# All value products and projections of ten loops as 64-row pairs

## The chip, the cores and the metric

One core of one Trainium2 chip runs the kernel. The metric is the device time in microseconds of one execution; the time before is 328.2 us, the median of three runs (327.85 to 329.61).

## What is computed

Self-attention over a batch of 32 sequences of different lengths, 8 heads of 64 channels, 512 channels in all. Rows past a sequence's length stay zero.

```
batch, max_seq, n_heads, head_dim = (32, 512, 8, 64)
for b in range(batch):
    x_b = x[b, :lengths[b]]
    q, k, v = np.split(np.matmul(x_b, w_qkv), 3, axis=-1)   # then by heads
    scores = scale * np.matmul(q, k.transpose(0, 2, 1))
    attn = softmax(scores)                                  # over the keys
    output[b, :lengths[b]] = np.matmul(attn, v)
```

## The kernel before

The sequences are sorted on the chip by length and taken two at a time. For each width N in `LOOPS` (512, 448, then 384 down to 96 in steps of 32) there is a loop; it takes the pairs whose longer sequence fits in N columns, so the lengths decide how often each body runs. A body has two positions, j = 0 and 1, one for each sequence of the pair. With the lengths of these inputs the loops from 512 to 96 run 1, 1, 1, 3, 1, 1, 1, 2, 1, 2, 1 and 1 times. n = ceil(N/128) is the number of 128-row tiles of a sequence.

A position does two things at once: the attention of its own sequence and the projections of the next one. Their order is written out by hand in `ORDER`, one string for each loop, with a bar between the two positions. A step's digit after "@" names PSUM banks (there are eight), and letters behind a colon name the engine of each copy out of PSUM: "a" is ScalarE (ACT), "d" is VectorE (DVE); a star says the same as "a". The steps are:

- `S#`: one group of scores, keys by queries. A head has 64 channels, so two heads are multiplied as a pair: two matmuls with 64 contraction rows each, on the upper and the lower half of the TensorE array, into two banks (line 1269; in the loop of 448 also 1259). ACT then takes the exponential of both banks in one instruction (line 1287).
- `B#a`, `B#b`, `B#c`: projections of q and k. The 128 contraction rows are cut in halves; the two halves of a column block go as a pair into two banks, first one way round, then the other, so that both banks get both halves (`halves`, line 1323). The copies follow the last part (line 1367).
- `U#a`, `U#b`: values of two tiles in the same manner (copies at line 1386). `V#a`, `V#b`: values of one tile, its 512 columns in two halves (copies at 1400). `W#a`, `W#b`: the same for the last half tiles of both sequences together.
- `Q#`, `K#`, `V#`, `W#` without a letter behind: projections with all 128 contraction rows in one matmul (`project`, line 300; `values`, line 311; `last_values`, line 1210).
- `A#` without a letter: the product of exponentials and values, 128 rows at once, 65 columns (64 channels and the row sum), `av`, line 1517 (line 1583 in the loops of 128 and 96, `at_once`). DVE then takes the reciprocal of the sums, sets dead rows to zero and scales: R, U, O at lines 1706, 1712, 1715. `Z#` (line 1557) adds the last half tile, as pairs.
- `A#a`, `A#b`: `paired`, line 1631. Two value products go together, each cut in 64-row halves, into two banks, in two rounds. Where the two banks are neighbours, `both_normed` does one R, U, O for both (lines 1671, 1680, 1693).
- `L`: DVE marks the live rows. `P`: DVE writes a mask and POOL casts the sequence after the next to 16 bits (line 371, n instructions). `D`: SyncE (SP) loads a later sequence into the buffer that the cast has read. `X`: SP transposes the cast sequence by DMA (line 328, n transfers); it waits for the projections of its own position, since it writes the buffer that they read, and the position after the next reads it. `E0` (`columns_left`): projections of columns left over when a loop runs again; its copies are replaced by a memset (line 1479) in a loop's last pass.

Instructions run in order on each engine. `plan_waits` works out the semaphore waits from what each step reads and writes; `op.skip < 0` marks `E0`.

Of the kernel before, what the change touches and what calls it, by code (L numbers as in the profile page):

```python
# [18 lines left out]
P = 128  # L19
# [21 lines left out]
def plan_waits(head, bodies, entries, rare):  # L41
# [22 lines left out]
    def follow(chain):  # L64
        clock = defaultdict(lambda: defaultdict(int))
        seen = defaultdict(list)
        write, readers = {}, defaultdict(list)
        ahead = chain[0] == "head"
        came = -1 if ahead else chain[0]
        for at, v in enumerate(chain):  # L70
# [10 lines left out]
            for w, j, k, op in todo:  # L81
                b = -1 if v == "head" else 2 * (at - ahead) + (j or 0)
                mine = clock[op.eng]
                if op.skip and op.eng == "PE":
                    mine = defaultdict(int, mine)
# [64 lines left out]
                    learn(o)  # L150
                by = op.name if op.dma else op.eng
                count = (seen[by][-1]["count"] if seen[by] else 0) + 1
                after = dict(mine)
                after[by] = count
                o = {"name": op.name, "by": by, "count": count, "clock": after, "b": b}
                o |= {"dma": op.dma, "entry": j is None, "skip": bool(op.skip) and op.eng != "POOL" and not op.passed, "order": len(seen["all"])}
# [5 lines left out]
                    readers[r].append(o)  # L162
                for r in op.writes:
                    write[r] = o
                    readers[r] = []

    follow(["head"])
    for v in range(len(bodies)):
        follow([v, v, v])
        for u in reversed(range(v)):  # L170
            follow([u, v, v])
        follow(["head", v, v])
# [4 lines left out]
def kernel(  # L177
# [9 lines left out]
    B, MAXS, D = x.shape  # L187
# [15 lines left out]
    def ring(n, shape, dtype, name, pool=const):  # L203
# [32 lines left out]
    LOOPS = [512, 448, *range(384, 64, -32)]  # L236

    ORDER = {
# [40 lines left out]
    }  # L279

    NARROW = (512, 448, 384, 320, 288, 256, 192, 128)
# [1620 lines left out]
    def op_of(v, j, k):  # L1902
        return head[k] if v == "head" else (entries[v] if j is None else bodies[v][j])[k]
# [57 lines left out]
    for (v, j, k), todo in waits.items():  # L1961
        op = op_of(v, j, k)
# [81 lines left out]
    with tc.tile_critical():  # L2044
# [38 lines left out]
        for v, N in enumerate(LOOPS):  # L2083
# [17 lines left out]
            body, after = f"loop_{N}", f"after_{N}"  # L2101
            nc.br_lt(pair, ends[v], on_true=body, on_false=after)
            with nc.body(body):
# [6 lines left out]
                for j in range(2):  # L2110
                    for e in EN:
                        mine = [(k, op) for k, op in enumerate(bodies[v][j]) if op.eng == e]
# [54 lines left out]
```

## Time and profile before

| | us |
|---|---|
| median of the runs | 328.2 (327.85 to 329.61) |
| span of the profiled execution | 328.5 |
| PE busy | 311.6 |
| ACT busy | 262.6 |
| DVE busy | 197.7 |
| POOL busy | 101.9 |

Stretches of the span, from the first exponential of one loop to that of the next: 512 from 23.1 to 59.7, 448 to 93.0, 384 to 118.1, 352 (three passes) to 190.4, 320 to 211.7, 288 to 232.8, 256 to 247.4, 224 (two passes) to 275.5, 192 to 288.3, 160 (two passes) to 310.5, then 128 and 96 to the end. Before 23.1 the weights are loaded and cast, the lengths sorted and the first sequence projected.

How to read it: PE is the matmul itself and PEld its weight load, which runs beside other matmuls. Matmuls are pipelined, so the mean time of one is its latency, and the rate is read from the starts in the timeline or from the pieces of the chain that ended last. Shapes such as 64*128 are contraction rows by weight columns.

### The profile page before, as it was taken

To read this page: it belongs to the slowest core of one execution; us is meant where nothing else is said; L and a number is where in the kernel's file an instruction comes from. 1 tells how busy PE (TensorE), PEld (TensorE's weight loads), DVE (VectorE), ACT (ScalarE), POOL (GpSimd) and SP (SyncE) were. 2 spreads that over 40 slices of the span, in tenths; PEclk is the share of its full clock that TensorE was granted. 3 is DMA by queue.
4 is the path that set the end of the run, shared out by engine and by line. 5 is a ranking of instruction groups with operands and counts; after the bars stand their busy time and mean duration, and the time that the engine had idled before them with its cause. 6 is when DMAs were issued, how large, how long until landed. Compare 5 with 4: busy or idle time off the path is not lost.

```text
span 328.5 us, 13310 instructions
## 1 busy us (share of the span) xinstructions
PE 311.6 (95%) x5092; PEld 202.3 (62%) x5092; DVE 197.7 (60%) x635; ACT 262.6 (80%) x413; POOL 101.9 (31%) x148
## 2 busy tenths in 40 slices
PE   6899999999999999999999999999998999999980
PEld 4444645555655556556656657667777886777860
DVE  6777567566666646456455465545575565776853
ACT  4379999897878988988978989899867779687761
POOL 6448040324030330330231243043222224435320
PEclk9999999999999999999999999999999999999997
DMA  6984749395858999696676766857459857966651
GB/s 217 382 278 80 251 140 327 76 354 153 304 52 298 224 269 258 197 268 224 233 214 224 255 194 205 211 174 242 156 131 227 183 176 164 223 206 177 193 180 66
DMA packets 69449, 68.85 MB, mean 210 GB/s; under 512 B 40720, under 2 KB 40720, under 8 KB 69392
## 3 DMA queue, kind: packets, MB, share of 16 engines
q1 hardware_dynamic: 69344, 68.12, 71.4%
q8 instruction: 33, 0.54, 0.7%
q14 instruction: 24, 0.20, 0.2%
q10 hardware_dynamic: 48, 0.00, 0.0%
HBM read 25.17 MB, written 33.55 MB: 179 GB/s over the span
## 4 chain that ended last, share of the span: by engine, by line
PE 84%; DVE 5%; DMA 3%; issue 2%; ACT 2%; SPq 1%; POOL 1%; DVEq 0%; POOLq 0%; ACTq 0%
PE banks L1323 41%; PE banks L1269 13%; PE banks L1517 12%; PE banks L300 6%; PE banks L311 6%; PE banks L1631 2%; DMA xT<-x 2%; DMA x_nat<-in_x_dram 2%; PE banks L1210 1%; PE banks L1557 1%; DVE out_nat L1715 1%; DVE rcp L1712 1%; DVE out_nat L1693 1%; SPq L328 1%; ACT et L1287 1%
## 5 line engine op out<-in xcount | busy, mean ns | idle before, releaser
L1287 ACT ACTIVATE et<-banks 128x704 f16<-128x704 f32 (+8 forms) x256 | 198.8, 825 | 27.8 <-PE banks L1269 24.7
L371 POOL TENSOR_TENSOR x<-x_nat,mask 128x512 f16<-128x512 f32 x83 | 84.2, 1041 | 184.3 <-DVE mask L1052 174.9
L1323 PE MATMUL banks<-xT,w_r 64*128 64x352 f16 (+9 forms) x1536 | 127.8, 294 | 1.8 <-DMA xT<-x 1.2
L1323 PEld LDWEIGHTS banks<-xT,w_r 64*128 64x128 f16 x1536 | 68.7, 94 | 39.0 <-PE banks L1323 8.5
L1269 PE MATMUL banks<-qz,kT 64*128 64x352 f16 (+11 forms) x624 | 77.5, 294 | 2.6 <-issue 0.7
L1715 DVE TENSOR_TENSOR out_nat<-banks,rcp 128x256 f32<-128x256 f32 (+1 forms) x110 | 53.0, 482 | 3.8
L1367 DVE CAST qz<-banks 128x448 f16<-128x448 f32 (+6 forms) x47 | 26.4, 561 | 45.2 <-PE banks L1323 44.8
L1517 PEld LDWEIGHTS banks<-v_aug,et 128*128 128x128 f16 x1240 | 41.7, 97 | 13.5 <-issue 6.8
L1517 PE MATMUL banks<-v_aug,et 128*128 128x65 f16 x1240 | 47.1, 194 | 0.0
L1323 PE MATMUL banks<-w_r,xT 64*128 64x512 f16 (+1 forms) x368 | 46.6, 372 | 0.3 <-ACT v_aug L1489 0.3
L1269 PEld LDWEIGHTS banks<-qz,kT 64*128 64x128 f16 x624 | 28.1, 93 | 25.9 <-issue 7.1
L1706 DVE RECIPROCAL rcp<-banks 128x4 f32<-128x4 f32 (+1 forms) x112 | 20.3, 181 | 20.7 <-PE banks L1517 7.3
L311 PE MATMUL banks<-w_r,xT 128*128 128x512 f16 x104 | 26.9, 381 | 0.5 <-DVE xT L782 0.5
L1386 DVE CAST v_aug<-banks 128x512 f16<-128x512 f32 x25 | 16.6, 690 | 17.9 <-PE banks L1323 17.9
L1323 PEld LDWEIGHTS banks<-w_r,xT 64*128 64x128 f16 x368 | 17.2, 94 | 14.1 <-PE banks L1323 1.0
L1367 ACT CAST kT<-banks 128x352 f16<-128x352 f32 (+6 forms) x47 | 22.5, 479 | 1.5 <-PE banks L1323 1.5
L300 PE MATMUL banks<-xT,w_r 128*128 128x160 f16 (+3 forms) x256 | 23.0, 243 | 0.5 <-DVE v_aug L1489 0.5
L1367 DVE CAST kT<-banks 128x352 f16<-128x352 f32 (+5 forms) x33 | 17.9, 552 | 7.7 <-PE banks L1323 7.6
L300 PEld LDWEIGHTS banks<-xT,w_r 128*128 128x128 f16 x256 | 16.6, 98 | 5.2 <-DMA xT<-x 0.6
L1367 ACT CAST qz<-banks 128x352 f16<-128x352 f32 (+6 forms) x33 | 15.3, 465 | 3.7 <-PE banks L1323 3.6
L1489 ACT CAST v_aug<-banks 128x512 f16<-128x512 f32 x15 | 8.8, 589 | 9.5 <-PE banks L311 9.5
L1631 PE MATMUL banks<-v_aug,et 64*128 64x65 f16 x624 | 14.2, 190 | 0.6 <-issue 0.6
(116 smaller groups left out, 193.3 us busy)
## 6 DMA issues: line engine op xcount, KB each, us to landing
x_nat<-in_x_dram SPq DMA_DIRECT2D x12, 768.0 KB, 6.4
out_dram<-out_nat SPq DMA_DIRECT2D x12, 768.0 KB, 4.0
x_nat<-in_x_dram SPq DMA_DIRECT2D x14, 512.0 KB, 4.5
out_dram<-zeros SPq DMA_DIRECT2D x12, 512.0 KB, 3.6
out_dram<-out_nat SPq DMA_DIRECT2D x12, 512.0 KB, 4.7
out_dram<-out_nat SPq DMA_DIRECT2D x4, 1024.0 KB, 7.0
x_nat<-in_x_dram SPq DMA_DIRECT2D x3, 1024.0 KB, 5.3
out_dram<-zeros SPq DMA_DIRECT2D x4, 768.0 KB, 4.7
```

The source lines that it names most:

```text
L300: last = nc.tensor.matmul(dst[:, 0:N], w_r[:, c, w0 : w0 + P], xT[:, c, 0:N], start=(c == 0), stop=(c == NC - 1),)
L311: last = nc.tensor.matmul(pv, xT[:, c, t * P : (t + 1) * P], w_r[:, c, 2 * D : 3 * D], start=(c == 0), stop=(c == NC - 1),)
L371: return engine.tensor_tensor(out=x16, in0=x32, in1=live.broadcast_to([P, D]), op=ALU.mult)
L1269: last = nc.tensor.matmul(psc[par][:, x * wide : x * wide + N], kT[r, i, c0 : c0 + P], qz[r, i, 0:N], start=True, stop=True,)
L1287: return nc.scalar.activation(out=et[:, :, x0:x1, 0:N], in_=got.rearrange("p j (x q) -> p j x q", q=wide)[:, :, x0:x1, 0:N], func=AF.Exp, ...
L1323: last = nc.tensor.matmul(to, lhs(rows, c), rhs(rows, c), start=(c == 0 and opens), stop=(c == NC - 1 and not opens),)
L1367: return lambda copy, bank: copy(out=buf[:, ms, 0:M], in_=bank[:, 0 : gm * M].rearrange("p (m q) -> p m q", q=M),)
L1386: return lambda copy, bank: copy(out=v_bufs[o][:, t, :, 0:HD], in_=bank.rearrange("p (h d) -> p h d", d=HD))
L1517: last = nc.tensor.matmul(pav[:, g, qt, :], e_bufs[e][:, c0 + qt * P : c0 + (qt + 1) * P], v_aug[:, kt, h, :], start=(kt == 0 and not (hal ...
L1631: last = nc.tensor.matmul(pavs[own][:, g, qt, :], e_bufs[e][rows, c0 + qt * P : c0 + (qt + 1) * P], (v_bufs[0] if ending else v_aug)[rows, ...
L1706: return nc.vector.reciprocal(out=rcp, in_=pav[:, :, :, HD])
L1715: return nc.vector.tensor_tensor(out=o_t[:, 0:n, h0 * HD : (h0 + heads) * HD].rearrange("p t (g d) -> p g t d", d=HD), in0=pav[:, :, :, 0:HD],
```

## The change

The strings of all loops are rewritten. In the ten loops from 512 to 160 every step without a letter is gone: `A#`, `Q#`, `K#`, `V#`, `W#` and `Z#` become `A#a`/`A#b`, `B#`, `U#`, `V#a`/`V#b` and `W#a`/`W#b`. Only `E0` keeps 128 rows. The order, the banks and the copy engines are new throughout, `P` and `D` stand later, and the loops of 128 and 96 keep their kinds of steps in another order. In `plan_waits` two lines change, both for TensorE steps under `skip < 0`, which is `E0` alone: such a step no longer passes on what it has waited for, and it no longer clears the list of readers of its bank.

```
-                after = dict(mine)
+                after = dict(clock[op.eng] if op.skip < 0 else mine)
...
                     write[r] = o
-                    readers[r] = []
+                    if op.skip >= 0 or op.eng != "PE":
+                        readers[r] = []
...
-        352: "L P D S0@56 V2*@4 S1@01 U0a@27 S2@56 S3@34 U0b:dd S4@01 B1a@65 S5@34 B1b:aa S6@01 A0@2 A2@7 "
-        "S7@34 B2a@56 S8@01 B2b:aa S9@34 B3a@27 B0a@10 S10@56 B3b:dd S11@34 B0b:ad A4@6 X A6@5 | L P D "
-        "S0@01 B0a@42 S1@67 B0b:da S2@01 B2a@53 S3@67 B3a@42 S4@01 B3b:da S5@67 B2b:da S6@01 A0@4 S7@67 "
-        "U0a@25 S8@01 S9@34 U0b:ad B1a@10 S10@67 S11@34 B1b:ad A2@5 A4@7 A6@3 V2*@0 X",
...
-        160: "L P S0@01 S1@23 V0@5 Q0*@4 A0@0 K0*@7 A2@1 S2@23 Z0 K2*@6 Q2*@7 X D A4@5 A6@2 Z4 | L P S0@34 "
-        "S1@67 K2@0 Q2*@1 A0@3 W0*@4 Q0@6 A2@5 K0*@0 Z0 S2@12 V0*@6 X D A4@4 A6@7 Z4",
...
+        352: "L S5@01 S8@23 B0a@54 B0b:dd S2@01 S10@67 U0a@32 S11@01 U0b:dd S4@45 S0@67 B1a@01 B1b:dd S6@45 B3a@32 "
+        "S3@67 B3b:ad S1@01 B2a@45 S9@67 B2b:da S7@01 P A0a@23 A0b D V2a@76 V2b:aa X A1a@45 A1b | L S7@67 "
+        "B1a@32 S0@01 B1b:ad S5@67 P V2a@54 V2b:ad S1@01 B0a@23 S4@56 B0b:dd S11@01 B2a@47 S3@56 B2b:ad S9@12 "
+        "U0a@03 S2@45 S8@67 U0b:da S10@12 A0a@45 S6@67 D A0b B3a@03 B3b:da A1a@67 A1b X",
...
+        160: "L S1@67 V0a@10 P V0b:ad D S0@23 B1a@67 B1b B1c:aa B0a@54 A0a@23 A0b S2@01 B0b B0c:ad A1a@01 X A1b | "
+        "L S2@56 S1@34 B1a@27 B1b P B1c:dd W0a@60 W0b:dd B0a@45 S0@12 B0b B0c:da D V0a@60 V0b:aa A1a@23 A1b "
+        "A0a@45 X A0b",
```

67 rows, old and new, of the table ORDER are left out of this document.

## The prediction

> **What bounds the kernel now.** I read the page first: the busy times and the chain that ended last.
>
> ```profile
> span 328.5 us, 13310 instructions
> ...
> PE 311.6 (95%) x5092; PEld 202.3 (62%) x5092; DVE 197.7 (60%) x635; ACT 262.6 (80%) x413; POOL 101.9 (31%) x148
> ...
> PE 84%; DVE 5%; DMA 3%; issue 2%; ACT 2%; SPq 1%; POOL 1%; DVEq 0%; POOLq 0%; ACTq 0%
> PE banks L1323 41%; PE banks L1269 13%; PE banks L1517 12%; PE banks L300 6%; PE banks L311 6%; PE banks L1631 2%; DMA xT<-x 2%; DMA x_nat<-in_x_dram 2%; PE banks L1210 1%; PE banks L1557 1%; DVE out_nat L1715 1%; DVE rcp L1712 1%; DVE out_nat L1693 1%; SPq L328 1%; ACT et L1287 1%
> ```
>
> TensorE is the bound, then: 84% of the chain is matmuls, and no other engine holds more than 5%. So the question is what TensorE's time consists of. The waits of TensorE, longest first, say little of it (the second stands at the very end of the span):
>
> ```profile
> PE banks L1323 <- DMA xT<-x: 1.2, 1, 1.2
> PE banks L1583 <- ACT et L1287: 1.0, 1, 1.0
> PE banks L1269 <- issue: 0.7, 3, 0.2
> PE banks L1631 <- issue: 0.6, 1, 0.6
> ```
>
> The chain of waits over a part of the 448 loop shows where matmuls lose time without a wait. Columns: start, time on the chain, what.
>
> ```profile
> 71.60 0.19 PE banks L1269 x2
> 71.79 0.84 PE banks L1517 x24
> 72.63 0.29 PE banks L1269 x2
> 72.92 0.12 PE banks L1557 x8
> 73.05 0.97 PE banks L311 x4
> 74.02 0.72 PE banks L1517 x24
> 74.74 0.23 PE banks L1557 x8
> ```
>
> L1269 and L1557 use 64 contraction rows, L1517 and L311 use 128. The 24 matmuls of L1517 take 0.72 us behind L311, which has 128 rows too, but 0.84 behind a 64-row step. Two score matmuls take 0.19 among their own kind and 0.29 behind L1517. The eight of L1557 take 0.12 behind a 64-row step and 0.23 behind a 128-row one. Each change between the two forms, in either direction, costs 0.10 to 0.12 us that no engine is waited for. I take 0.10, the score matmuls' figure and the least of the three.
>
> **The change part by part.** *Changes of form removed.* I walked along the old strings with the number of passes and counted neighbours of different form: 16 in the 512 loop, 22 in 448, 12 in 384, 30 in three passes of 352, 7 in 320, 4 in 288, 2 in 256, 3 in two of 224, 5 in 192, 16 in two of 160, 3 in 128, 4 in 96: 124. That 352 runs three times is seen from its exponentials (72 of 128x704, which is 3 x 24). In the new strings only the entry into the 512 loop and the loops of 128 and 96 have any: 10. `E0` would add some, but the loops that have it run once on these lengths, so its other arm, the memset of line 1479, runs each time and no left-over projection does:
>
> ```profile
> L1287 ACT ACTIVATE et<-banks 128x704 f16<-128x704 f32 x72 | 52.1, 765 | 3.5 <-PE banks L1269 2.9
> L1479 DVE MEMSET kT<- 128x64 uint32 x6 | 0.7, 112 | 0.6 <-PEq L2005 0.6
> L1479 DVE MEMSET kT<- 128x128 uint32 x2 | 0.3, 165 | 0.0
> ```
>
> So 114 changes of form go: 114 x 0.10 = **-11.4 us**. The bounds are 0.09 (-10.3) and 0.12 (-13.7). This lies on the bounding engine, with no cover over it.
>
> *Value products.* 1232 of the 1240 matmuls of L1517 (eight stay in the 128 loop) become 2464 of half the rows. Views: groups by form, the timeline of TensorE and the chain, in the 320 loop.
>
> ```profile
> L1517 PE MATMUL banks<-v_aug,et 128*128 128x65 f16 x1240 | 47.1, 194 | 0.0
> L1631 PE MATMUL banks<-v_aug,et 64*128 64x65 f16 x624 | 14.2, 190 | 0.6 <-issue 0.6
> ```
>
> ```profile
> 196.61 0.71 PE L1631 MATMUL banks<-v_aug,et 64*128 64x65 f16 x36
> 197.16 0.31 PE L1269 MATMUL banks<-qz,kT 64*128 64x320 f16 x2
> ```
>
> The 36 halves start at 196.61 and the next step at 197.16: 0.55/36 = 15.3 ns for a half, 30.6 for a pair, against 0.72/24 = 30.0 to 30.3 ns for a whole one. The sum: 2464 x 15.3 = 37.7 us after, 1232 x 30.3 = 37.3 before, **+0.4 us**; with 15.5 ns for a half it is +0.9, and with 15.2 it is nothing.
>
> The Trainium skill, "TensorE: Matmul & The Clock Gate", section "Wait — 56ns, not 53.3ns?", speaks against this step: it says that starts of matmuls are never less than about 25 ns apart, however few columns. By that figure, as an estimate, the halves would cost 2464 x 25 = 61.6 us, 24 more than the whole ones. The trace disagrees for halves on different rows, with 15.3 ns, and the trace decides.
>
> *Projections.* 76 matmuls of L311, 40 of L1210 and 128 of L300 (all of the 160 loop) become pairs. Chain of waits in the loops of 352, 160 and 192:
>
> ```profile
> 135.49 0.86 PE banks L1323 x8
> ...
> 140.76 0.86 PE banks L311 x4
> ```
>
> ```profile
> 300.75 0.55 PE banks L300 x8
> ```
>
> ```profile
> 281.43 0.55 PE banks L1323 x16
> ```
>
> Eight halves of 512 columns take as long as four whole ones (0.86), sixteen halves of 160 columns as long as eight whole ones (0.55). So 0; W has half the columns in twice the matmuls and lies between these two. A bound of 1% either way on these 20 us is 0.2.
>
> *Copies and norms.* By the strings ACT's copies fall from 131 to 85 and DVE's rise from 117 to 183. DVE gains half of its R, U, O steps back. In a position of 352, DVE gets three casts more, 3 x 0.52 = 1.6, and does two large norms instead of four small ones: 4 x (0.19 + 0.17 + 0.56) = 3.7 becomes 2 x (0.20 + 0.17 + 1.0) = 2.7. The O of 128x768 is not in the trace; it lies between 0.69 (128x512) and 1.11 (twice 128x384), and 1.0 is in proportion.
>
> ```profile
> L1715 DVE TENSOR_TENSOR out_nat<-banks,rcp 128x384 f32<-128x384 f32 x48 | 26.7, 557 | 1.6
> L1706 DVE RECIPROCAL rcp<-banks 128x6 f32<-128x6 f32 x48 | 9.1, 190 | 12.1 <-PE banks L1631 5.5 <-PE banks L1517 5.3 <-PE banks L1557 0.6
> L1712 DVE TENSOR_TENSOR rcp<-rcp,v_aug 128x6 f32<-128x6 f32 x32 | 5.4, 169 | 1.1
> L1693 DVE TENSOR_TENSOR out_nat<-banks,rcp 128x512 f32<-128x512 f32 x12 | 8.3, 691 | 0.4
> L1367 DVE CAST qz<-banks 128x352 f16<-128x352 f32 x14 | 7.3, 524 | 15.7 <-PE banks L1323 15.7
> ```
>
> Windows over the two positions of a 352 pass (after the span: PE, PEld, DVE, ACT, POOL, each busy time and count):
>
> ```profile
> 118.10:130.00 11.90, 11.90 (x183) 7.31 (x183) 5.53 (x16) 10.77 (x20) 3.04 (x3) 1.00 1.03 254
> 130.00:142.20 12.20, 12.20 (x182) 7.11 (x179) 7.14 (x23) 10.57 (x19) 3.04 (x3) 1.00 0.84 217
> ```
>
> TensorE is busy all through at full clock. DVE goes from 5.5 to about 6.1 of 11.4 us: hidden under TensorE, **0**. Uncovered, it would be the 0.6 of each position, 4 us over the six.
>
> *P and D later.* The mask, n casts, the load and, behind it on SP, the transposes move back. The load is read two positions later, 11 us in the 160 loop (four positions from 288.3 to 310.5); the cast needs 3.04 of a 352 position. Cost **0**, covered by TensorE's work of a whole position; what happens without the cover is the third rival. *The two lines in the planner* touch only `E0`; they can lengthen the waits around a step that doesn't run: 0, at most 0.5 either way. *New orders and banks* make new waits and drop old ones; the trace can't show them. I keep the sum of small waits as it is, with about 4.5 us to either side: that is near what the waits of the loops add up to, and half of what the changes of form make up in the loops down to 288 (below).
>
> **Sum**: 328.5 - 11.4 + 0.4 = 317.5 us for the profiled execution. It ran 0.3 us above the median of the runs, so the time is **317.2 us**.
>
> **The rivals.** *The waits go as well* (0.15). The pairs leave TensorE with one form, `Z` steps with their own banks vanish, and the late-transpose wait of 1.2 us, the two of 0.7 and 0.6 and smaller ones in the loops, some 4.5 us in all, fall away with the new orders: 317.2 - 4.5 = 312.7. Against it: the loops that were already mostly pairs kept such waits.
>
> *ACT becomes the bound* (0.14). In a 352 position ACT is busy 10.8 of 11.9 us. The new first position ends with S7, A0, V2, A1: 72 halves, 1.1 us, then 0.86, then 1.1 again, 3.1 us in which ACT has one exponential (0.76) and two half copies (0.38 each), so it stands idle for some 1.6 us.
>
> ```profile
> L1386 ACT CAST v_aug<-banks 128x512 f16<-128x512 f32 x19 | 10.7, 590 | 0.6 <-PE banks L1323 0.5
> L1367 ACT CAST kT<-banks 128x352 f16<-128x352 f32 x17 | 7.9, 463 | 0.0
> L1400 ACT CAST v_aug<-banks 128x256 f16<-128x256 f32 x2 | 0.6, 378 | 0.7 <-PE banks L1323 0.7
> ```
>
> Five copies of 0.46 and one of 0.59 become two of 0.46 and two of 0.38: 1.2 us less. 10.8 - 1.2 + 1.6 = 11.2, just under TensorE's new 11.9 - 0.5 = 11.4. If ACT comes out a little longer, TensorE waits for banks. The loops from 512 to 288 hold 91 of the changes of form, 9 us; half lost is 4.5: 321.7. For it: how close both sums are. Against it: the exponentials are spread so that TensorE runs ahead of ACT by one or two groups.
>
> *Late transposes, slower* (0.04). Place: the two-tile loops from 256 to 160, six pairs, 12 positions of 5 to 8 us. There X must wait for the position's last projection, now nearer its end, and for a cast that starts later; SP needs 1.26 us for each transpose, and under load they land late:
>
> ```profile
> L328 SPq DMA_TRANSPOSE xT<-x x74: 1181/1256/2499, 26.1 to 314.5; - x74
> ```
>
> ```profile
> 248.70 5.64 DMA xT<-x
> 254.34 0.14 issue
> ```
>
> That transpose made TensorE wait 1.2 us at the start of the 224 loop. If each of the 12 positions waited so, it would be 14.9 us: 317.2 + 14.9 = 332. From 11.0 / 12 = 0.92 us in each, the change wins nothing. Against it: the chain has this wait once in 12 positions, and X has a position's slack.
>
> *Halves one after the other, slower* (0.01). A pair is worth its price only while its two halves run together. If in the new long runs (144 halves in a row at the end of 384) each half cost what a whole one does, it would be 2464 x (30.3 - 15.3) = 37 us: 354. From 15.3 + 11.0 / 2464 us = 19.8 ns each the gain is gone. The run of 36 shows nothing of it. The Trainium skill's rule of 25 ns, above, would be this case.
>
> *The gain is eaten exactly* (0.02), between the second and third: 328. The form of the forecast, within about 2 us, has the remaining 0.64.
>
> **How the numbers follow.** Predicted is the likeliest case, 317.2. The range takes in the first two rivals with the small bounds around them (AV +0.5, planner 0.5): 312.0 to 322.5. About 0.5% is what a measurement of this kernel can tell from no change. Faster: 0.64 + 0.15 + 0.14 = 0.93; within 0.5%: 0.02; slower: 0.04 + 0.01 = 0.05.
>
> **What would show it.** In the profile after: no L1517 row but the eight of the 128 loop, no L1210, L1557, L300 beyond the head and the last two loops; L1631 at 3264 matmuls (624, the 2464, and the 176 of `Z`) at 15 ns by their starts; score matmuls at 0.15 and 0.19 on the chain behind value products. A 352 pass takes 23.1 us instead of 24.1. TensorE stays near 95% and its share of the chain grows. The forecast is wrong if ACT's part of the chain rises beyond 10%, if DMA xT<-x leads the waits, or if the halves stand more than 16 ns apart.

## The result, and the profile after

The changed kernel takes 365.5 us, the median of four runs (364.28 to 368.30), against 328.02 us for the kernel before (four runs, 327.83 to 329.61): a ratio of 1.114, with a 95% interval of 1.109 to 1.119. It is 37 us slower, where 11 us faster was forecast. In the changed kernel most source lines stand one further on: L1324 is the projection of `halves`, L1270 the scores, L1632 the value product of `paired`, L1288 the exponential.

The page of the changed kernel: the span, the busy times, the instruction queue (q8, its packets counted first), the chain that ended last and the row of the value products.

```profile
span 363.8 us, 16325 instructions
...
PE 327.8 (90%) x6688; PEld 208.2 (57%) x6688; DVE 208.8 (57%) x536; ACT 245.4 (67%) x367; POOL 101.9 (28%) x148
...
q8 instruction: 42, 0.69, 0.8%
...
PE 86%; issue 6%; ACT 3%; DVE 3%; DMA 1%; POOL 0%; SPq 0%; POOLq 0%; ACTq 0%; PEldq 0%; DVEq 0%
...
L1632 PE MATMUL banks<-v_aug,et 64*128 64x65 f16 x3264 | 70.5, 190 | 8.3 <-issue 4.9
```

The instruction queue in the page of before:

```profile
q8 instruction: 33, 0.54, 0.7%
```

No other engine became the bound: ACT and DVE hold 3% of the chain each, and ACT is busy 17 us less than before. What grew is "issue", time in which TensorE waits for nothing that the profile shows, from 2% to 6%, and TensorE's own time. The 3264 value matmuls are there as forecast.

The waits of TensorE's weight loads, first before, then after (time in all, times, longest):

```profile
PEld banks L1323 <- PE banks L1323: 9.9, 36, 0.4
```

```profile
PEld banks L1324 <- PE banks L1324: 36.7, 114, 0.6
PEld banks L1632 <- PE banks L1632: 9.9, 54, 0.2
```

TensorE's weight loads wait for TensorE's own matmuls: 36 times before, 168 times after. The timeline of TensorE in the first pass of the 352 loop shows what one costs (start, time, what):

```profile
137.74 0.31 PE L1270 MATMUL banks<-qz,kT 64*128 64x352 f16 x2
137.89 1.50 PE L1632 MATMUL banks<-v_aug,et 64*128 64x65 f16 x72
139.23 1.28 PE L1324 MATMUL banks<-w_r,xT 64*128 64x256 f16 x16
140.34 1.50 PE L1632 MATMUL banks<-v_aug,et 64*128 64x65 f16 x72
```

The 72 halves of `A0a A0b` start at 137.89 and the next step at 139.23: 1.34 us, where 72 x 15.3 ns are 1.10. The 0.23 us over lies between the two rounds of the step. The first round puts the halves of two products into two banks one way round, the second the other way round. The planner is told to wait in between: `after=begun[-1]` in the two helpers, and in `plan_waits` the lines `if op.after: needs.append(seen[op.after][-1])`, one of the few cases in which TensorE waits for its own earlier work. In the old strings a score step or another step always stood between the rounds, so most of the wait was covered. In the new ones 115 second rounds (counted with the passes: 50 of A, 41 of B, 16 of V, 5 of U, 3 of W) stand directly behind their first.

The second loss shows in the timeline of the 448 loop, in a run of 168 halves:

```profile
75.37 2.23 PE L1632 MATMUL banks<-v_aug,et 64*128 64x65 f16 x119
78.81 1.17 PE L1632 MATMUL banks<-v_aug,et 64*128 64x65 f16 x49 [1.21 <-issue]
```

TensorE stops for 1.4 us in the middle of a step, and nothing releases it but "issue". In the queues over 76 to 77.4 us, just before, a packet of instructions is under way:

```profile
q8 instruction: 1, 0.02, 4.3%
```

That packet lands at 77.50, and TensorE goes on at 78.81. The waits of TensorE after, those named issue and one that stands among them in the view:

```profile
PE banks L1632 <- issue: 4.9, 5, 2.1
PE banks L1270 <- DVE out_nat L1694: 4.0, 2, 2.5
...
PE banks L1324 <- issue: 1.9, 2, 1.7
PE banks L1270 <- issue: 1.8, 5, 0.5
```

With the value matmuls doubled the profile has 3015 instructions more (16325 against 13310), and the instruction queue fetches 42 packets instead of 33. TensorE runs out of instructions in and behind dense runs of halves, in the changed kernel where they are executed for the first time. The stops recur at the same place in the program: behind the 3135th weight load or matmul of TensorE in the changed kernel and in experiments 1, 2, 5 and 10, behind the 4350th in the changed kernel and in experiments 2 and 5. The 2.5 us put down to `out_nat` begin at 124.6 us, 0.1 us after such a packet set out, and belong here too by the fifth experiment, where the stop at the same place is named issue.

For the account below I took the distances between starts of successive matmuls from 23 us on, less what the same matmul or pair takes undisturbed. Of what is left, 0.097 us goes to each change of form, the 0.2 to 0.3 us between the rounds of a step to the rounds, and every other gap over 0.06 us to other waits. The gaps sorted as rounds are 118, three more than the 115 that the strings have; which these three are was not followed up.

| us from 23 us on | before | after |
|---|---|---|
| matmuls by their columns | 270.3 | 270.7 |
| changes of form (count) | 11.9 (123) | 0.9 (9) |
| between adjacent rounds (count) | 0 (0) | 27.2 (118) |
| other waits, missing instructions among them | 12.8 | 31.3 |

The changes add up to 0.4 - 11.0 + 27.2 + 18.5 = 35.1 us, and the spans differ by 35.3. So the gain that was forecast is there, and two losses stand on top of it.

### The profile page after: what moved, and what is told of

Read it like the earlier page. It is cut to its first block, busy times and chain, and to the rows that moved or that the text cites. A ratio compares the mean times of both kernels' runs of the same rounds, so it can differ in the third digit from the quotient of the medians.

```text
span 363.8 us, 16325 instructions
## 1 busy us (share of the span) xinstructions
PE 327.8 (90%) x6688; PEld 208.2 (57%) x6688; DVE 208.8 (57%) x536; ACT 245.4 (67%) x367; POOL 101.9 (28%) x148
## 4 chain that ended last, share of the span: by engine, by line
PE 86%; issue 6%; ACT 3%; DVE 3%; DMA 1%; POOL 0%; SPq 0%; POOLq 0%; ACTq 0%; PEldq 0%; DVEq 0%
PE banks L1324 51%; PE banks L1632 16%; PE banks L1270 12%; PE banks L301 3%; ACT et L1288 2%; PE banks L312 2%; DMA x_nat<-in_x_dram 1%; DVE v_aug L1387 1%; DVE out_nat L1694 1%; PE banks L774 0%; ACT v_aug L1490 0%; DVE kT L823 0%; PE banks L1260 0%; PE banks L1584 0%; ACT v_aug L1401 0%
## 5 line engine op out<-in xcount | busy, mean ns | idle before, releaser
L1288 ACT ACTIVATE et<-banks 128x704 f16<-128x704 f32 (+8 forms) x256 | 199.3, 821 | 69.0 <-PE banks L1270 63.5
L1324 PE MATMUL banks<-xT,w_r 64*128 64x352 f16 (+9 forms) x1792 | 144.7, 287 | 4.7 <-issue 1.7
L1324 PEld LDWEIGHTS banks<-xT,w_r 64*128 64x128 f16 x1792 | 75.4, 94 | 50.4 <-PE banks L1324 24.9
L1270 PE MATMUL banks<-qz,kT 64*128 64x352 f16 (+11 forms) x624 | 78.8, 297 | 8.8 <-DVE out_nat L1694 4.0
L1632 PE MATMUL banks<-v_aug,et 64*128 64x65 f16 x3264 | 70.5, 190 | 8.3 <-issue 4.9
L1632 PEld LDWEIGHTS banks<-v_aug,et 64*128 64x128 f16 x3264 | 60.6, 94 | 21.8 <-PE banks L1632 9.9
L1324 PE MATMUL banks<-w_r,xT 64*128 64x512 f16 (+1 forms) x640 | 70.0, 338 | 2.0 <-DVE v_aug L1387 0.4
L1368 DVE CAST qz<-banks 128x352 f16<-128x352 f32 (+6 forms) x66 | 36.2, 549 | 51.1 <-PE banks L1324 51.0
L1694 DVE TENSOR_TENSOR out_nat<-banks,rcp 128x512 f32<-128x512 f32 (+1 forms) x67 | 52.7, 787 | 2.3
L1270 PEld LDWEIGHTS banks<-qz,kT 64*128 64x128 f16 x624 | 28.6, 95 | 29.8 <-issue 6.7
L1324 PEld LDWEIGHTS banks<-w_r,xT 64*128 64x128 f16 x640 | 28.1, 95 | 28.4 <-PE banks L1324 10.2
L1368 DVE CAST kT<-banks 128x352 f16<-128x352 f32 (+6 forms) x63 | 34.0, 540 | 6.9 <-PE banks L1324 6.8
L1672 DVE RECIPROCAL rcp<-banks 128x8 f32<-128x8 f32 (+1 forms) x67 | 14.5, 216 | 38.5 <-PE banks L1632 36.5
L301 PE MATMUL banks<-xT,w_r 128*128 128x96 f16 (+2 forms) x128 | 12.6, 253 | 1.0 <-DVE v_aug L1490 0.5
```

Of the source, the lines that this page charges most:

```text
L301: last = nc.tensor.matmul(dst[:, 0:N], w_r[:, c, w0 : w0 + P], xT[:, c, 0:N], start=(c == 0), stop=(c == NC - 1),)
L1270: last = nc.tensor.matmul(psc[par][:, x * wide : x * wide + N], kT[r, i, c0 : c0 + P], qz[r, i, 0:N], start=True, stop=True,)
L1288: return nc.scalar.activation(out=et[:, :, x0:x1, 0:N], in_=got.rearrange("p j (x q) -> p j x q", q=wide)[:, :, x0:x1, 0:N], func=AF.Exp, ...
L1324: last = nc.tensor.matmul(to, lhs(rows, c), rhs(rows, c), start=(c == 0 and opens), stop=(c == NC - 1 and not opens),)
L1368: return lambda copy, bank: copy(out=buf[:, ms, 0:M], in_=bank[:, 0 : gm * M].rearrange("p (m q) -> p m q", q=M),)
L1632: last = nc.tensor.matmul(pavs[own][:, g, qt, :], e_bufs[e][rows, c0 + qt * P : c0 + (qt + 1) * P], (v_bufs[0] if ending else v_aug)[rows, ...
```

## The experiments

Theory S says that the waits between adjacent rounds are the main loss. Theory F says that missing instructions are a loss of their own. Their rivals are the new order itself, with its other waits, and halves that are slow in themselves.

**1. Rounds apart.** In the changed kernel one more step is put between all 115 adjacent rounds; here the first position of 352.

```
-S5@01 S8@23 B0a@54 B0b:dd S2@01 S10@67 ... A0a@23 A0b D V2a@76 V2b:aa X A1a@45 A1b
+S5@01 S8@23 B0a@54 S2@01 B0b:dd S10@67 ... A0a@23 V2a@76 A0b D A1a@45 V2b:aa X A1b
```

> The changed kernel with one more matmul step put between the two rounds of a pair step wherever they stood next to each other (115 places, no place left); same steps, banks and copy engines. Theory S (seam): a second round directly behind the first costs 0.23 us, since it writes the same two banks from the other half of the rows; a single score step between hides 0.12 to 0.21 of it. So 115 x 0.16 to 0.23 = 18 to 26 us less than 365.5: 339 to 347. Rival F (TensorE is fed too slowly with instructions, whose number rose by 3200): the same instructions in almost the same order, so no change, 363 to 367.

Measured: 366.06 us, ratio 1.117 (1.112 to 1.122). Missed. The waits between adjacent rounds fell as planned, from 118 to 4 (27.2 to 1.0 us), but the other waits rose from 31.3 to 58.8 us. The view of waits names the new ones:

```profile
PEld banks L1296 <- PE banks L1296: 17.2, 62, 0.4
PEld banks L1604 <- ACT et L1260: 10.9, 22, 1.1
PEld banks L1296 <- ACT et L1260: 6.8, 15, 0.9
PEld banks L1242 <- ACT et L1260: 6.7, 19, 0.7
```

(L1296 is the projection here, L1604 the value product, L1242 the scores, L1260 the exponential.) A score step is 0.15 us long and leaves 0.08 to 0.11 of the 0.23 uncovered, and a step that moves brings its copies and its exponentials to other places, so that TensorE then waits for ACT. The test moved two things at once; it shows that these moves don't mend the order. The time itself is what rival F had forecast (363 to 367), but not for its reason, since the waits between rounds did go and others took their place; so it decides nothing between S and F.

**2. Rounds that don't cross.** The wait stays, but each row half keeps its bank in both rounds, so that one half of the contraction is added twice and the other left out.

```
-    z = half ^ turned
+    z = half
...
-    i, side = h // 2, half * (own ^ j ^ turned)
+    i, side = h // 2, half * (own ^ j)
```

> The changed kernel, where the second round of each pair step keeps the first one's row halves for each bank instead of crossing them; it adds one half of the contraction twice and leaves the other out. Same count and order of instructions. Theory S: the 0.23 us between adjacent rounds go wholly, 115 x 0.23 = 26 us: 339. Rival F, or any cost of the order of steps: unchanged, 363 to 367.

Measured: 366.58 us, ratio 1.118 over the same batch's 327.78. Missed: 117 waits of 27.0 us in all are still there, and the weight loads wait as before.

```profile
PEld banks L1324 <- PE banks L1324: 36.6, 114, 0.6
PEld banks L1632 <- PE banks L1632: 10.4, 57, 0.2
```

So the price is that of the wait, and not of two row halves that swap banks.

**3. The kernel before, with adjacent rounds.** In the 352 loop alone, the ten second rounds of U and B stand directly behind their first.

```
-B0a@42 S1@67 B0b:da S2@01 B2a@53 S3@67 B3a@42 S4@01 B3b:da S5@67 B2b:da
+B0a@42 B0b:da S1@67 S2@01 B2a@53 B2b:da S3@67 B3a@42 B3b:da S4@01 S5@67
```

> The kernel before, where in the 352 loop alone the second round of U and B stands directly behind the first (10 places in a pass, 30 in three passes). Theory S: 30 x 0.23 = 6.9 us more, less about 2 us that single score steps between rounds leave uncovered before: 328.0 + 5 = 333, and 2 us for each pass of the 352 loop. Rival: adjacency costs nothing of its own, 327 to 329.

Measured: 350.13 us, ratio 1.067 (1.063 to 1.071), 22 us slower; the time forecast, 333, is missed by 17. The 30 rounds (ten in each of three passes) cost 6.86 us, 0.229 each, as in the changed kernel, so S holds for the price. The rest, some 15 us, was not foreseen: with the copies of the projections moved, ACT comes late and TensorE waits for it in each pass. The longest row of that kind (L1489 is the value product here, L1259 the exponential):

```profile
PEld banks L1489 <- ACT et L1259: 10.6, 19, 1.3
```

**4. Whole value products, waits kept.** In the changed kernel each round of `paired` multiplies one product with all 128 rows into its own bank; the places in the order, the banks and the waits stay.

```
-    for own in range(2):
-        last = nc.tensor.matmul(pavs[own][:, g, qt, :], e_bufs[e][rows, ...], v_aug[rows, kt, h, :], ...)
+    h = both[own] + g
+    last = nc.tensor.matmul(pavs[own][:, g, qt, :], e_bufs[e][:, ...], v_aug[:, kt, h, :], ...)
```

> The changed kernel, where the two rounds of a value product are two products with 128 rows, one for each bank, in the same places (the last half tiles stay 64-row pairs): 2464 halves become 1232 whole matmuls. Theory S alone: 50 seams of value products less, -11.5 us, 148 more changes of form at 0.097, +14.4: 368. Theory F beside it (the stalls of 0.5 to 2.3 us in the middle of value products, which no semaphore explains, are TensorE waiting for instructions): these stalls go too, some 8 us less: 360, with about 33 instruction packets on queue 8 instead of 42.

Measured: 363.59 us, ratio 1.109. The changes of form are back (157, 15.2 us), and yet it is no slower than the changed kernel. The instruction queue is back at 33 packets, and no stop inside a value product is left; of the waits named issue this is the longest row:

```profile
PE banks L1270 <- issue: 1.2, 4, 0.4
```

The expectation took the waits inside the value products as gone. They stayed, since the planner's wait was kept:

```profile
PEld banks L1626 <- PE banks L1626: 10.5, 58, 0.2
```

So S alone comes to 365.5 + 14.3 = 380 us, not 368, and the measured 363.6 is 16 us less. The halves of the value products bring as much loss by missing instructions, with the slower clock behind the longest stops (last section), as they save in changes of form, and F is worth about twice the 8 us expected of it. That 363.6 lies between the two times forecast is chance.

**5. Not crossed, no wait.** Experiment 2 without the wait, `after=""` in both helpers.

> As the run with rounds that don't cross (each bank gets the same row half in both rounds, one half of the contraction twice, the other left out), and now also without the planner's wait of the second round on the first (the 'after' of a pair step), which nothing needs when no bank changes its row half. Theory W: the 0.23 us between adjacent rounds are this wait, TensorE waiting until its own first round has ended. 118 x 0.23 = 27 us go: 339. Rival: the cost lies in the array or the banks and not in the wait: 366, as before.

Measured: 345.96 us, the median of three runs (343.44 to 346.42; a fourth took 351.94), ratio 1.051 (1.047 to 1.055), 21 us less than experiment 2. It is far from the rival's 366 and 7 us above the 339 forecast. The rounds cost 1.3 us now (6 left). But TensorE, with no waits to slow it, runs out of instructions all the more:

```profile
PE banks L1632 <- issue: 10.3, 7, 2.8
PE banks L1270 <- issue: 6.1, 6, 4.6
PE banks L1324 <- issue: 2.3, 1, 2.3
```

That is 18.7 us. In experiment 2, which differs by the wait alone, the same name has 11.5 us (8.6 in the changed kernel); the clock was 0.973 over the span, 0.987 in both others. The two losses hide each other in part, which is why 339 was too low.

**6. Whole value products without the wait between them.** Experiment 4, `after` left out in `paired` alone. Two whole products into two banks need no wait, so that the computation is the full one.

> As the run with whole value products, and without the wait between a value product's two products, which now go to different banks. Theory W: 50 waits of 0.23 us less, 363.6 - 11.5 = 352. Rival: 363 to 364.

Measured: 350.7 us, ratio 1.069, 12.9 us less than experiment 4. A hit.

**7. The kernel before, with wider gaps.** If the wait is 0.23 us, the rest of 0.08 behind a single score step might be won in the kernel before. In the loops from 384 to 288 the second round moves one more step back in 15 places (23 with the passes, where the expectation says 21).

```
-S4@01 B1a@65 S5@34 B1b:aa S6@01 A0@2
+S4@01 B1a@65 S5@34 S6@01 B1b:aa A0@2
```

> The kernel before, where in the loops of 384 to 288 a second round of B, U or W that stands behind a single score step goes one step further back, 21 places counted with the passes. Theory W: a score step of 0.12 to 0.16 us leaves 0.07 to 0.11 us of the wait uncovered, so up to 21 x 0.09 = 1.9 us less, 326 against 327.8, if the later copies hold nothing up. Rival: other waits take their place, 327.8 or more.

Measured: 335.83 us, ratio 1.025 (1.023 to 1.027): slower, where 326 us was hoped for and the rival had 327.8 or more. ACT's share of the chain rises from 2% to 11%: the late copies cost more than the rests that they save.

**8. No waits between rounds, whole value products.** The order, banks and copy engines of the changed kernel, but with neither of the two losses: the value products of experiment 6, and for B, U, V and W the uncrossed rounds without a wait of experiment 5, which leave out one half of the contraction.

> The changed kernel with whole value products and with rounds of B, U, V and W that don't cross, and no wait between rounds anywhere (the projections add one half of the contraction twice and leave out the other). Theories W and F together: 366 - 27 (118 waits) - 17 (stalls that went with the halves) + 14 (148 changes of form) = 336. Rival: the new order itself costs the rest, 350 or more.

Measured: 331.64 us, ratio 1.012 (1.010 to 1.013), 4 us less than the 336 forecast. No rounds cost anything, 33 packets, and the other waits are 11.2 us (12.8 before). There are 34 changes of form more than in the kernel before, 3.3 us; without them it would stand at 328.3. So the new order, freed of its waits, stands level with the old one, whose waits are still in its time, and the rival that had the order itself at 350 or more falls. The loss lies in the waits between rounds and in the missing instructions, with the clock that falls behind the longest stops.

**9 and 10. The halves put back in some loops.** Experiment 8, with halves again in the value products of one stage.

```
-op(title, "PE", lambda: matmuls(turned), ...)
+op(title, "PE", lambda: (matmuls_halves if N == 352 else matmuls)(turned), ...)
```

(N in (512, 448) in the tenth.)

> The kernel with whole value products and no waits (331.6 us), with one thing put back: in the loop of 352 alone the value products are halves again, in the same uncrossed rounds without waits. As in that kernel one half of the contraction is added twice and the other left out in the pair steps, so that only its time is read. The loop runs three times; its 10 changes of form per pass go, 30 x 0.097 = 2.9 us. Theory F (halves are as cheap as whole ones, and what costs time is that TensorE runs out of instructions the first time a part of the code is run): the second and third pass are each about 1.0 us shorter than in the kernel with whole products, any wait named issue stands in the first pass, and the time is 328.7 plus 0 to 2: 328.7 to 330.7. Theory H (halves in long runs cost more wherever they stand): no pass is shorter, 331.6 or more, and the second and third pass show the loss as well as the first.

> The same kernel (331.6 us) with the halves put back in the loops of 512 and 448 alone, each of which runs once; again one half of the contraction is added twice and the other left out in the pair steps. 16 changes of form go in each loop by a count of the strings, 32 x 0.097 = 3.1 us. Theory F: these loops hold some 500 matmuls more, all run for the first time, so waits named issue come back in them; with the halves in all loops they were 4.2 us here: 331.6 - 3.1 + 4.2 = 332.7, no gain at all, between 331 and 334, and more packets in the instruction queue than 33. If halves bring no waits for instructions here, 328.5. Theory H: as F or longer, but with the loss spread over the halves and no waits named issue.

Measured in 352: 330.09 us, ratio 1.006 (1.004 to 1.008). Windows over the three passes (span, TensorE's busy time and count, and so on; clock, DMA share and rate at the end), with whole products (experiment 8) and with halves:

```profile
117.95:141.75 23.80, 23.80 (x388) 15.91 (x386) 13.71 (x31) 19.84 (x33) 6.07 (x6) 1.00 0.72 173
141.75:165.55 23.80, 23.80 (x388) 15.81 (x386) 13.75 (x31) 19.84 (x33) 6.07 (x6) 1.00 0.88 249
165.55:189.41 23.86, 23.85 (x388) 15.84 (x386) 13.82 (x32) 19.84 (x34) 6.27 (x7) 1.00 0.78 236
```

```profile
117.99:141.20 23.21, 23.07 (x532) 16.19 (x530) 13.80 (x32) 19.98 (x34) 6.07 (x6) 1.00 0.74 175
141.20:164.39 23.19, 23.07 (x532) 16.18 (x530) 13.77 (x31) 19.98 (x34) 6.07 (x6) 1.00 0.86 240
164.39:187.67 23.28, 23.05 (x532) 16.18 (x530) 13.79 (x32) 19.98 (x34) 6.28 (x7) 1.00 0.79 241
```

All three passes gain 0.6 us. Halves are not slow in themselves, so theory H falls; the time is within F's 328.7 to 330.7, though the gain is less than the 1.0 us per pass that the changes of form are worth, and no wait for instructions came even in the first pass.

Measured in 512 and 448: 337.38 us, ratio 1.027 (1.023 to 1.031), 5.7 us slower than experiment 8, although 32 changes of form went; missed, since F had 331 to 334. The queue has 37 packets, and the waits inside the value products are back:

```profile
PE banks L1667 <- issue: 4.8, 3, 2.5
```

So the same halves win in one stage and lose in another. F has the right cause and too small a size: it left out that the clock falls behind a long stop, as it did here from 62.8 to 66.3 us, to 0.50.

## Why the prediction was wrong

**Changes of form removed, -11.4 us: right.** 123 became 9, 11.9 us became 0.9. Experiments 4, 6 and 8 show the other side, with 157 of them at 15.2 us.

**Value products, +0.4 us: the price per half was right.** In the runs of halves of the changed kernel, of up to 87, the starts are 15.1 ns apart on the mean (3141 distances). The matmuls by their columns grew by 0.4 us, as worked out. The rival with halves one after the other did not occur, although its 354 us was the nearest of the times given, and the rule of 25 ns in the Trainium skill, "TensorE: Matmul & The Clock Gate", section "Wait — 56ns, not 53.3ns?", isn't borne out for halves on different rows.

**Projections, 0: right for the matmuls, wrong for the step.** I priced eight halves at 0.86 us from a place where the rounds stand apart, and took the price into an order where they don't. With `B#a B#b` side by side it is 0.23 more.

**New orders and banks, the sum of small waits kept, with 4.5 us to either side: this is the step that failed.** It was mis-sized by a factor of ten: the rounds took 27.2 us and the other waits 18.5 more. "The trace can't show them" was untrue for the first part. The row of weight loads that wait for the same line, 36 times, stood in the waits of before, and the chain of waits of before, in the 352 loop, has the rest of such a wait behind a single score step:

```profile
129.92 0.60 PE banks L1323 x8
130.52 0.15 PE banks L1269 x2
130.67 0.69 PE banks L1323 x8
```

The second round takes 0.69 us instead of 0.60, although a score step of 0.15 lies between it and the first: a wait of about 0.24 us, of which 0.15 is covered. Counting neighbouring rounds in the new strings as I counted neighbours of different form gives 115, and 115 x 0.24 = 28 us. The order was described in the prediction's own words ("72 halves, 1.1 us, then 0.86, then 1.1 again") without the seam inside each. Two readings in the prediction were a little off, and nothing hangs on them: its list of waits, longest first, lacks the longest, 1.9 us for `h_ones` before the first loop, and the wait for a transpose stands at the second position of the 224 loop, not at its start.

The Trainium skill has a rule that fits this wait: in "TensorEngine Tiling (Array Packing)", section "Gotcha 1: PSUM Pressure", different row tiles cannot access the same PSUM bank at once, and software must see to it. No run here crosses its rounds without the wait, so that it is needed is not shown. I weighed a rule on the spacing of matmuls and missed this one. It gives no price; here it is 0.228 us a round.

**What no step had: instructions as a resource.** I counted the matmuls' time, not their number. The changed kernel has 3192 weight loads and matmuls more on TensorE, and each 16 KB packet of them is used up in half the time in a run of halves. Experiments 4, 5 and 10 show that this binds. One sign of it stood in the trace of before, in the row "L1631 <- issue: 0.6" that the prediction quotes and counts among the small waits that may fall away. It is a stop of the same kind, inside a run of halves in the 192 loop, with a packet of the instruction queue landed at 284.05:

```profile
284.66 0.41 PE L1631 MATMUL banks<-v_aug,et 64*128 64x65 f16 x15
285.70 0.19 PE L1631 MATMUL banks<-v_aug,et 64*128 64x65 f16 x1 [0.63 <-issue]
```

The three rows named issue come to 8.6 us in the changed kernel, 7.3 more than the two of before, and the 2.5 at 124.6 us belong to them. Two spells of 3.4 us at half the clock (last section) cost up to 1.7 us each, 3.4 in all. Together that is some 13 of the 18.5 us; the remainder is spread over small waits, most of them 0.3 to 0.5 us at the ends of positions.

**Copies, P and D later, the planner's two lines: 0, borne out** by experiment 8, where the order with all of them, but without the waits, stands level with the one before.

**The rivals.** ACT as the bound: 3% of the chain, against the 10% named. The late transposes are not among the leading waits. "The waits go as well" is what experiments 9 and 5 show in part: with the waits left out, the 352 pass takes 23.2 us, and 23.1 was forecast for the whole change. The full changed kernel has this pass:

```profile
155.09:180.64 25.55, 24.91 (x532) 15.49 (x530) 14.67 (x31) 20.14 (x34) 6.08 (x6) 1.00 0.87 215
```

The 2.36 us over 23.19 are eight adjacent rounds of 0.228 and seven rests of 0.09 behind single steps: 2.45. In the passes after the first, the account closes with the rounds alone; between 152.8 and 210.0 us no packet of instructions was fetched.

**What stays open.** Why the halves in 352 find their instructions in time and those in 512 and 448 don't was not settled; the packets of a loop depend on what else has been fetched by then. Nor was it tested why packets come too late; the single packet is not slower than before (0.9 to 1.7 us in both kernels). Whether the wait between rounds could be made shorter, with the full computation, was not tried. No version that ran beats the kernel before: the fastest with the full computation was experiment 7, at 335.83 us.

## What to carry to other kernels

Where a step is cut in rounds that must not overlap, the price of the step is that of the work between its rounds too: look for an engine that waits for itself in the waits of before, and count how often the new order puts such rounds side by side. A change that doubles the number of short instructions for the same work should be counted in instructions as well, since the fetch of the program can bind where the work does not. And in an order that is tuned by hand, a loss seen in one place (here 0.08 us behind a step) may not be had by moving a step, because its copies move with it: in experiments 1, 3 and 7 steps were moved, and TensorE then waited for ACT.

## What the runs showed of the hardware

**Instruction fetch can stop TensorE in straight code.** Stops of 0.8 to 4.8 us stand inside or behind long runs of halves, each with a packet of the instruction queue under way or landed just before; TensorE went on 1.2 to 1.8 us after the landing, 1.3 in the case shown (77.50 to 78.81). A run of halves takes 15 ns for a weight load and a matmul, whole products 30 ns for the same two. The Trainium skill, "Runtime: NRT & Kernel Launch", section "Instruction fetch mechanics", calls the crossing of a 16 KiB boundary "mostly hidden"; the trace agrees for the kernel before, with 33 packets and one wait named issue inside a value product, of 0.6 us, and not for the dense halves of the changed kernel.

**A stop of 2 to 3 us can halve the clock.** The granted clock of the changed kernel is 1.00 or 0.50. Apart from the start and the end of the span, it is 0.50 in two spells, from 128.7 and from 255.0 us, each 3.4 us long: behind the stop at 124.6 us, which lasted 2.6 us, and behind two at 251.4 and 253.8 us, of 2.3 and 1.7 us.

```profile
128.70:132.10 3.40, 3.40 (x24) 1.33 (x20) 0.96 (x2) 1.76 (x4) 0.00 (x0) 0.50 0.60 229
255.00:258.40 3.40, 2.84 (x26) 1.72 (x28) 0.64 (x2) 1.94 (x2) 0.00 (x0) 0.50 0.55 204
```

The last figures but two are the clock. Half the speed for 3.4 us costs 1.7 us where TensorE is busy all through. The length of a stop alone does not decide: in the changed kernel the stops of 1.4 us at 77.4 and of 2.0 us at 217.4 left the clock at 1.00. In experiment 5 a stop of 2.1 us at 74.7 and one of 4.8 us at 120.7 were followed by 0.50, the second for 6.8 us, while those of 2.5 us at 208.9 and of 3.0 us at 300.3 were not:

```profile
76.90:80.30 3.40, 3.40 (x71) 2.70 (x67) 2.35 (x9) 0.92 (x1) 0.00 (x0) 0.50 0.61 66
124.70:131.50 6.80, 6.01 (x38) 3.34 (x40) 0.96 (x2) 3.08 (x5) 0.00 (x0) 0.50 0.61 193
208.80:216.00 7.20, 4.84 (x77) 3.33 (x75) 3.37 (x12) 4.73 (x10) 3.04 (x3) 1.00 0.51 137
300.00:310.00 10.00, 6.70 (x204) 6.01 (x200) 4.42 (x15) 5.49 (x12) 2.93 (x4) 1.00 0.64 155
```

The Trainium skill, "TensorE: Matmul & The Clock Gate", section "What's actually happening", has the clock halved after an idle window of about 3.4 us; the half agrees, but here shorter stops, of 2.1 and 2.6 us, were followed by it.
